# Second MLP product of an encoder block: half of the row-tile pairs by seven block products, two of the four weight sums formed by an accumulating load

## The chip, the cores and the metric

The kernel runs on one core of a Trainium2 chip. The metric is the device time of one execution in microseconds (us); smaller is better. The core has five engines that run beside each other, each with a queue of its own that it works through in order: PE (matrix products, accumulating in PSUM banks of 128x512 floats), DVE and ACT (elementwise work), POOL (GpSimd, elementwise work and issuing transfers) and SP (issues transfers). Transfers between HBM and the on-chip buffers run on 16 DMA engines.

## The reference

One post-norm encoder block on 256 tokens of width 2048, in float32:

```
mix = hybrid_mixer(x, ...)                                  # two kinds of attention
x = layer_norm(ALPHA * x + mix, ln1_g, ln1_b)
x = layer_norm(ALPHA * x + cross_attention(x, mem), ln2_g, ln2_b)
ff = square(relu(x @ w_mlp_in)) @ w_mlp_out                 # 2048 -> 8192 -> 2048
x = layer_norm(ALPHA * x + ff, ln3_g, ln3_b)
```

The change lies wholly in the MLP, and there in the product with `w_mlp_out`: a 256x8192 activation times an 8192x2048 matrix.

## The kernel before

**Precision.** Each product of two float32 matrices is made by three PE passes. Both operands are split into a high part (a copy in the type fp32r, made by ACT, L80) and a low part (the rest, source minus high part, made by DVE, L81); `mm3` (L146 to L148) adds high x high, high x low and low x high into one PSUM bank. So each 1024 columns of a weight cost one ACT and one DVE instruction before PE can use them. The split weights live in tiles `w_hi` and `w_lo` with four buffers each.

**The MLP.** The 8192 hidden columns are worked off in NCH = 4 chunks of CH = 16 column tiles of 128. Per chunk, four calls of `hidden_group` (L760) make the hidden activations `ht` (PE lines L195 and L200, then `hidden`, L730, squares and splits them). Then `pair_product(c, q)` (L804) multiplies the chunk's activations with the matching 2048 rows of `w_mlp_out`, for the left (q = 0) and the right (q = 1) half of the 2048 output columns. There are seven such calls: the last chunk's right half is made in another way (`proj_tokens`), so that the tail is short.

**Units.** A pair product runs over eight units p = 0 to 7. Unit p is a pair of row tiles (256 rows) by 1024 columns of the weight, laid out in HBM as one block of 128 partitions x 2048 floats, in the order B12, B11, B22, B21 of its four 128x512 blocks. The activation pair is a 2x2 block matrix A too (two token blocks by two row tiles). A plain unit makes all eight block products: 24 matmuls of 512 columns, into the banks x11, x12, x21, x22. It splits the weight in two parts of 1024 columns (`part`, L796). A unit for which `strassen(p)` holds (L745: p = 3 and p = 7) uses the Strassen-Winograd scheme: seven block products, 21 matmuls, of which four go to banks p1, p5, p6, p7 of their own. It needs four sums of activation blocks (s1 to s4 in `hidden`, L736 to L743: four DVE instructions on 128x128 and one split of 128x512 into `sums_h`) and four sums of weight blocks in a tile `s` of 2048 columns:

- columns 0 to 1023: B11 + B12 and B22 + B12, made by one DVE instruction over 1024 columns (L789),
- columns 1024 to 1535: (B11 + B12) + B22, one DVE instruction over 512 columns (L789),
- columns 1536 to 2047: that plus B21, one more over 512.

It splits four parts: `raw[512:1536]`, `raw[1536:2048]`, `s[0:1024]` and `s[1024:2048]`, that is 3584 columns in place of 2048. After the last unit, banks p1, p5, p6, p7 are copied out by ACT (L852) and added into the result rows `res` by DVE (L841, L844, L847).

**Loads.** `load_unit` (L775) takes the next unit: one transfer of 1 MB on SP's queue (L782). Units 0, 1, 4, 5 go to the two halves `raw2` of a fixed tile `wx`, the others to the three buffers of `raw`, which the first MLP product also uses. The two slots `sums_w` for `s` are the other half of `wx`. Two units are loaded ahead in program order.

**Order.** The tile framework plans the order of each engine's queue ahead of the run, from its own estimates of durations, within the dependencies; an instruction then waits at the head of its in-order queue until its inputs are there. Small DVE work that may wait is put in a list `side`: weight sums, the last additions into `res`, statistics. Each `part` takes one entry off it (`pump`), and a Strassen unit empties it first (L822).

Of the kernel before, what the change touches and what calls it, by code (L numbers as in the profile page):

```python
# [12 lines left out]
F32R = mybir.dt.float32r  # L13
BF16 = mybir.dt.bfloat16
AF = mybir.ActivationFunctionType
ALU = mybir.AluOpType
AX = mybir.AxisListType

P = 128
# [14 lines left out]
CH = 16  # L34
# [4 lines left out]
def encoder_kernel(ctx: ExitStack, tc: tile.TileContext, t, out):  # L39
    nc = tc.nc  # L40
# [19 lines left out]
    def f(ap):  # L60
        return ap.bitcast(F32)
# [7 lines left out]
    def tmp_tile():  # L69
        return tmp.tile([P, 512], F32, tag="tmp", name="tmp")  # L70
# [4 lines left out]
    def pin(ins, pinned):  # L75
        return tc.keep_in_program_order(ins) if pinned else ins

    def split(hi, lo, src, scale=None, pinned=False):
        if scale is None:
            pin(nc.scalar.activation(hi, src, AF.Copy), pinned)  # L80
            return pin(nc.vector.tensor_tensor(out=lo, in0=src, in1=f(hi), op=ALU.subtract), pinned)  # L81
        else:
            nc.scalar.activation(hi, src, AF.Copy, scale=scale)
            nc.vector.scalar_tensor_tensor(
                out=lo, in0=src, scalar=scale, in1=f(hi), op0=ALU.mult, op1=ALU.subtract)
# [9 lines left out]
    side = deque()  # L95

    def pump(n=1):

        for _ in range(n):
            if side:  # L100
                side.popleft()()
# [43 lines left out]
    def mm3(ps, ah, al, bh, bl, start, stop):  # L145
        nc.tensor.matmul(ps, ah, bh, start=start, stop=False)  # L146
        nc.tensor.matmul(ps, ah, bl, start=False, stop=False)  # L147
        nc.tensor.matmul(ps, al, bh, start=False, stop=stop)  # L148
# [289 lines left out]
    for b in range(NB):  # L438
# [3 lines left out]
        a, c, e = krn[:, 0:64], krn[:, 64:128], krn[:, 256:512]  # L442
        nc.vector.tensor_tensor(out=a, in0=v, in1=krt[:, 0, b, :], op=ALU.mult)
        for i in range(2):
            j = 1 - i
            nc.vector.tensor_tensor(out=c[:, i * 32:(i + 1) * 32], in0=v[:, j * 32:(j + 1) * 32],
                                    in1=krt[:, 1, b, i * 32:(i + 1) * 32], op=ALU.mult)
        nc.gpsimd.memset(e, 0.0)
        for par in range(2):
            dst = e[:, par * P:(par + 1) * P].rearrange("p (i g c) -> p i g c", g=2, c=32)  # L450
            nc.vector.tensor_tensor(
                out=dst[:, :, par, :], in0=a.rearrange("p (i c) -> p i c", c=32),
                in1=c.rearrange("p (i c) -> p i c", c=32), op=ALU.add)
# [41 lines left out]
    def stats_tile():  # L495
        return [small.tile([P, 5, 6], F32, tag="bn", name="bn"), 0]
# [81 lines left out]
    def big3(name):  # L578
        return big.tile([P, 8192], F32R, tag="big", name=name).rearrange("p (k c) -> p k c", c=512)
# [132 lines left out]

    early.close()
    late = ctx.enter_context(tc.tile_pool(name="late", bufs=1))
    s_in = Stream(t["w_mi"][4:])
    sts = [stats_tile() for _ in range(NB)]
    ht = big3("ht")
    sums_h = late.tile([P, 2048], F32R, name="sums_h").rearrange("p (u l c) -> p u l c", l=2, c=512)
    wx = big.tile([P, 8192], F32, tag="big", name="wx")
    raw2, sums_w = [[wx[:, o:o + 2048] for o in (i, i + 2048)] for i in (0, 4096)]  # L720

# [8 lines left out]
    def hidden(ps, j):  # L730

        r = []
        for i in range(2):
            r.append(square(ps[i]))
            split(ht[:, j + i, 0:S], ht[:, j + i, S:2 * S], r[i])
        if strassen(j // 2):  # L736
            (a11, a21), (a12, a22) = [(x[:, 0:P], x[:, P:S]) for x in r]
            s = tmp_tile()
            s1, s2, s3, s4 = [s[:, o:o + P] for o in range(0, 4 * P, P)]
            for o, a, b, op in ((s1, a21, a22, ALU.subtract), (s3, a11, a21, ALU.subtract),  # L740
                                (s2, s1, a11, ALU.subtract), (s4, a12, s2, ALU.add)):
                nc.vector.tensor_tensor(out=o, in0=a, in1=b, op=op)
            split(sums_h[:, j // 8, 0, :], sums_h[:, j // 8, 1, :], s)  # L743

    def strassen(p):  # L745
        return p % 4 == 3

    def last_weights(k):

# [10 lines left out]
    def hidden_group(nexts, tiles, j0):  # L760
# [7 lines left out]
        for i in range(0, G, 2):  # L768
# [1 line left out]

    units = [(c, q, p) for c in range(NCH) for q in range(2) for p in range(CH // 2)
             if not (c == NCH - 1 and q == 1)]
    loaded = deque()

    def load_unit(chunk):  # L775

        if not units or units[0][0] != chunk:
            return
        c, q, p = units.pop(0)
        seven = strassen(p)  # L780
        raw = raw2[p % 4] if p % 4 < 2 else raw_tile()
        nc.sync.dma_start(raw, t["w_mo"][(c * 2 + q) * (CH // 2) + p])  # L782
        s = None
        if seven:
            s = sums_w[p // 4 % 2]
            b12, b22, b21 = [raw[:, o:o + 512] for o in (0, 1024, 1536)]

            def add(out, a, b):
                side.append(lambda: nc.vector.tensor_tensor(out=out, in0=a, in1=b, op=ALU.add))  # L789
            add(s[:, 0:1024].rearrange("p (i c) -> p i c", i=2), raw[:, 512:1536].rearrange("p (i c) -> p i c", i=2),  # L790
                b12[:, None, :].broadcast_to([P, 2, 512]))
            add(s[:, 1024:1536], s[:, 0:512], b22)
            add(s[:, 1536:2048], s[:, 1024:1536], b21)
        loaded.append((raw, s))

    def part(src):  # L796
        w = src.shape[1]
        hi = wsp.tile([P, 1024], F32R, tag="w_hi", name="w_hi")
        lo = wsp.tile([P, 1024], F32R, tag="w_lo", name="w_lo")
        split(hi[:, :w], lo[:, :w], src)  # L800
        pump()
        return [(hi[:, o:o + 512], lo[:, o:o + 512]) for o in range(0, w, 512)]

    def pair_product(c, q):  # L804

        x11, x12, x21, x22 = [acc_tile() for _ in range(4)]
        p1, p5, p6, p7 = [att_tile() for _ in range(4)]
        n = CH // 2
        for p in range(n):
            load_unit(c)  # L810
            raw, s = loaded.popleft()
            k = 2 * p

            def a(k_, b):
                return ht[:, k_, b * P:(b + 1) * P], ht[:, k_, S + b * P:S + (b + 1) * P]

            def sm(i):
                return (sums_h[:, p // 4, 0, i * P:(i + 1) * P], sums_h[:, p // 4, 1, i * P:(i + 1) * P])

            if strassen(p):  # L820
                first, last = p == 3, p == n - 1
                pump(len(side))  # L822
                for src, todo in ((raw[:, 512:1536], ((p1, a(k, 0), first), (x12, sm(3), False))),
                                  (raw[:, 1536:2048], ((x11, a(k + 1, 0), False),)),
                                  (s[:, 0:1024], ((p5, sm(0), first), (p7, sm(2), first))),
                                  (s[:, 1024:2048], ((p6, sm(1), first), (x21, a(k + 1, 1), False)))):
                    for (hi, lo), (ps, (ah, al), start) in zip(part(src), todo):
                        mm3(ps, ah, al, hi, lo, start, last)
            else:
                for i in range(2):  # L830
                    w = part(raw[:, i * 1024:(i + 1) * 1024])
                    for (hi, lo), to in zip(w, ((x12, x22), (x11, x21))):
                        for b in range(2):
                            ah, al = a(k + i, b)
                            mm3(to[b], ah, al, hi, lo, p == 0 and i == 0, to[b] is x22 and p == n - 2 and i == 1)
        cols = [slice((2 * q + i) * 512, (2 * q + i + 1) * 512) for i in range(2)]
        r11, r12, r21, r22 = [res[b][:, cc] for b in range(NB) for cc in cols]

        def first_add(r, ps):
            if c == 0:  # L840
                nc.vector.scalar_tensor_tensor(out=r, in0=r, scalar=ALPHA, in1=ps,  # L841
                                               op0=ALU.mult, op1=ALU.add)
            else:
                nc.vector.tensor_tensor(out=r, in0=r, in1=ps, op=ALU.add)  # L844

        def add(o, x, y, op=ALU.add):
            side.append(lambda: nc.vector.tensor_tensor(out=o, in0=x, in1=y, op=op))  # L847

        first_add(r22, x22)
        m1, m5, m7, m6 = [tmp_tile() for _ in range(4)]  # L850
        for m, ps in ((m1, p1), (m5, p5), (m7, p7), (m6, p6)):
            nc.scalar.activation(m, ps, AF.Copy)  # L852
        first_add(r12, x12)
        first_add(r11, x11)
        first_add(r21, x21)
        add(r22, r22, m5)
        add(r12, r12, m5)
        add(m6, m1, m6)
        add(m7, m6, m7)
        add(r11, r11, m1)  # L860
        add(r12, r12, m6, ALU.subtract)
        add(r21, r21, m7)
        add(r22, r22, m7, ALU.subtract)
        if c == NCH - 1:
            for b, r in ((0, r11), (0, r12), (1, r21), (1, r22)):
                side.append(lambda b=b, r=r: stats(sts[b], r))

    for c in range(NCH):
        for g in range(CH // G):
            first = c == 0 and g == 0  # L870
# [27 lines left out]
    for b in range(NB):  # L898
# [10 lines left out]
        for i, c in enumerate(cols):  # L909
            if i + 1 < len(cols):  # L910
                shift(cols[i + 1])
            pin(nc.vector.scalar_tensor_tensor(
                out=res[b][:, c], in0=res[b][:, c], scalar=r, in1=b3[:, c],
# [119 lines left out]
```

## Time and profile before

| | |
|---|---|
| median of 3 runs | 1113.58 us (1113.04 to 1114.1) |
| the profiled execution | 1112.53 us |
| its span, first to last instruction | 1110.8 us |
| mean granted PE clock | 0.995 |
| matmuls | 5962 |
| MLP second product, seven pair products | about 42.2 us each |

The profile is one execution. "Busy" is the time in which an engine executes something; a matmul's own duration is longer than its distance to the next one, since matmuls are pipelined, so distances are read from start times. "SPq" is the queue of transfers that SP issues. "Granted clock" is the share of full PE speed that the throttle allowed.

### The profile page before, as it was taken

To read this page: it belongs to the slowest core of one execution; us is meant where nothing else is said; L and a number is where in the kernel's file an instruction comes from. 1 tells how busy PE (TensorE), PEld (TensorE's weight loads), DVE (VectorE), ACT (ScalarE), POOL (GpSimd) and SP (SyncE) were. 2 spreads that over 40 slices of the span, in tenths; PEclk is the share of its full clock that TensorE was granted. 3 is DMA by queue.
4 is the path that set the end of the run, shared out by engine and by line. 5 is a ranking of instruction groups with operands and counts; after the bars stand their busy time and mean duration, and the time that the engine had idled before them with its cause. 6 is when DMAs were issued, how large, how long until landed. Compare 5 with 4: busy or idle time off the path is not lost.

```text
span 1110.8 us, 15234 instructions
## 1 busy us (share of the span) xinstructions
PE 1095.6 (99%) x5962; PEld 946.3 (85%) x5962; DVE 828.1 (75%) x1202; ACT 574.1 (52%) x842; POOL 38.3 (3%) x45
## 2 busy tenths in 40 slices
PE   9999999999999989999999999999999999999996
PEld 6988899888998878888888888888888888888885
DVE  6878677687888777876976667868667777667695
ACT  6555565546576344544554445455445545554550
POOL 1402000000100000000000000000000000000000
PEclk9999999999999999999999999999999999999998
DMA  9654454466477427655456555555554565555372
GB/s 335 234 224 152 152 190 149 155 227 241 177 216 277 146 82 268 226 189 208 171 190 227 189 190 189 184 195 196 203 187 173 190 232 189 186 190 191 113 258 83
DMA packets 37944, 215.86 MB, mean 194 GB/s; under 512 B 4336, under 2 KB 5232, under 8 KB 14192
## 3 DMA queue, kind: packets, MB, share of 16 engines
q1 hardware_dynamic: 37872, 214.89, 54.5%
q8 instruction: 46, 0.75, 0.3%
q14 instruction: 26, 0.21, 0.1%
HBM read 212.78 MB, written 2.10 MB: 193 GB/s over the span
## 4 chain that ended last, share of the span: by engine, by line
PE 98%; DVE 1%; DMA 0%; issue 0%; ACT 0%; POOL 0%; DVEq 0%; SPq 0%
PE acc L147 16%; PE acc L146 16%; PE acc L148 16%; PE att L195 11%; PE acc L195 11%; PE att L200 5%; PE acc L200 5%; PE att L148 2%; PE att L147 2%; PE att L146 2%; PE acc L188 2%; PE acc L186 2%; PE acc L187 2%; PE att L535 1%; PE att L350 1%; PE att L362 0%
## 5 line engine op out<-in xcount | busy, mean ns | idle before, releaser
L81 DVE TENSOR_TENSOR w_lo<-raw,w_hi 128x1024 fp32r<-128x1024 f32 (+2 forms) x318 | 367.0, 1162 | 180.1 <-ACT w_hi L80 178.6
L80 ACT ACTIVATE w_hi<-raw 128x1024 fp32r<-128x1024 f32 (+2 forms) x318 | 320.0, 1013 | 333.6 <-PE acc L148 154.2
L147 PE MATMUL acc<-w_lo,ht 128*128 128x512 f32 x396 | 154.0, 389 | 0.0
L148 PE MATMUL acc<-w_hi,ht 128*128 128x512 f32 x396 | 154.0, 389 | 0.0
L195 PE MATMUL att<-x2t,w_hi 128*128 128x512 f32 x512 | 139.6, 394 | 0.0
L146 PE MATMUL acc<-w_hi,ht 128*128 128x512 f32 x396 | 136.0, 389 | 0.0
L195 PE MATMUL acc<-x2t,w_hi 128*128 128x512 f32 x480 | 132.3, 394 | 0.0
L80 ACT ACTIVATE w_hi<-wx 128x1024 fp32r<-128x1024 f32 x84 | 87.9, 1061 | 80.5 <-PE acc L148 59.7
L81 DVE TENSOR_TENSOR w_lo<-wx,w_hi 128x1024 fp32r<-128x1024 f32 x84 | 100.9, 1221 | 34.5 <-ACT w_hi L80 33.6
L195 PEld LDWEIGHTS att<-x2t,w_hi 128*128 128x128 f32 x512 | 88.1, 189 | 12.3
L195 PEld LDWEIGHTS acc<-x2t,w_hi 128*128 128x128 f32 x480 | 82.6, 189 | 11.5
L146 PEld LDWEIGHTS acc<-w_hi,ht 128*128 128x128 f32 x396 | 74.3, 188 | 15.5
L147 PEld LDWEIGHTS acc<-w_lo,ht 128*128 128x128 f32 x396 | 74.3, 188 | 15.4
L148 PEld LDWEIGHTS acc<-w_hi,ht 128*128 128x128 f32 x396 | 74.3, 188 | 15.4
L200 PEld LDWEIGHTS att<-x2t,w_lo 128*128 128x128 f32 x512 | 77.5, 189 | 10.2
L200 PEld LDWEIGHTS acc<-x2t,w_lo 128*128 128x128 f32 x480 | 73.3, 189 | 9.5
L200 PE MATMUL att<-x2t,w_lo 128*128 128x256 f32 x512 | 80.2, 281 | 0.0
L200 PE MATMUL acc<-x2t,w_lo 128*128 128x256 f32 x480 | 77.0, 281 | 0.0
L147 PE MATMUL acc<-w_lo,xt 128*128 128x512 f32 (+2 forms) x192 | 69.2, 362 | 0.0
L148 PE MATMUL acc<-w_hi,xt 128*128 128x512 f32 (+2 forms) x192 | 69.2, 361 | 0.0
L146 PE MATMUL acc<-w_hi,xt 128*128 128x512 f32 (+2 forms) x192 | 65.6, 361 | 0.5 <-ACT w_hi L80 0.5
L148 PE MATMUL acc<-w_hi,ot 128*128 128x512 f32 (+1 forms) x136 | 51.9, 382 | 0.0
(243 smaller groups left out, 1789.2 us busy)
## 6 DMA issues: line engine op xcount, KB each, us to landing
raw<-in_w_mi SPq DMA_DIRECT2D x64, 1024.0 KB, 4.8
wx<-in_w_mo SPq DMA_DIRECT2D x28, 1024.0 KB, 4.9
raw<-in_w_mo SPq DMA_DIRECT2D x28, 1024.0 KB, 4.8
raw<-in_w_out SPq DMA_DIRECT2D x16, 1024.0 KB, 4.9
raw<-in_w_ml SPq DMA_DIRECT2D x8, 1024.0 KB, 4.9
raw<-in_w_b SPq DMA_DIRECT2D x5, 1024.0 KB, 4.9
raw<-in_w_qa SPq DMA_DIRECT2D x16, 256.0 KB, 5.4
raw<-in_w_qa SPq DMA_DIRECT2D x4, 1024.0 KB, 4.9
```

Source lines behind the costliest of these rows:

```text
L80: pin(nc.scalar.activation(hi, src, AF.Copy), pinned)
L81: return pin(nc.vector.tensor_tensor(out=lo, in0=src, in1=f(hi), op=ALU.subtract), pinned)
L146: nc.tensor.matmul(ps, ah, bh, start=start, stop=False)
L147: nc.tensor.matmul(ps, ah, bl, start=False, stop=False)
L148: nc.tensor.matmul(ps, al, bh, start=False, stop=stop)
L186: nc.tensor.matmul(ps, hi, xt[:, k, 0:S], start=k == 0, stop=False)
L187: nc.tensor.matmul(ps, hi, xt[:, k, S:2 * S], start=False, stop=False)
L188: nc.tensor.matmul(ps, lo, xt[:, k, 0:S], start=False, stop=k == nk - 1)
L195: nc.tensor.matmul(ps, hi[:, i * P:(i + 1) * P], xt[:, k, :], start=k == 0, stop=k == nk - 1)
L200: nc.tensor.matmul(ps[:, 0:S], lo[:, i * P:(i + 1) * P], xt[:, k, 0:S], start=False, stop=False)
L350: nc.tensor.transpose(pp[:, st * S + b * P:st * S + b * P + P], ev[:, b, st * P:(st + 1) * P], ident)
L535: nc.tensor.transpose(ps[:, o:o + P], x(b, k // 4)[:, (k % 4 + j) * P:(k % 4 + j + 1) * P], ident)
```

## The change

Of the eight units of a pair product, p = 1, 3, 5 and 7 are now made by seven block products, in place of 3 and 7. `sums_h` grows from two to four sets of activation sums. Of the four weight sums, the first two are no longer made by DVE: B12 is loaded twice side by side into `s[0:1024]` by SP, and then a transfer issued by GpSimd adds B11 and B22 from HBM onto it. `raw` then holds only columns 512 to 2047 for such a unit. The other two sums remain DVE additions over 512 columns; they go to a list `sums` of their own, of which each `part` takes one entry ahead of `side`, and a seven-product unit empties that list but no longer `side`. Three units rather than two are loaded ahead in program order.

```diff
+    SEVEN = ((1, 3, 5, 7), (1, 3, 5, 7))
-    sums_h = late.tile([P, 2048], F32R, name="sums_h").rearrange("p (u l c) -> p u l c", l=2, c=512)
+    sums_h = late.tile([P, 4096], F32R, name="sums_h").rearrange("p (u l c) -> p u l c", l=2, c=512)
...
-        if strassen(j // 2):
+        if j // 2 in SEVEN[0]:
...
-            split(sums_h[:, j // 8, 0, :], sums_h[:, j // 8, 1, :], s)
-
-    def strassen(p):
-        return p % 4 == 3
+            u = SEVEN[0].index(j // 2)
+            split(sums_h[:, u, 0, :], sums_h[:, u, 1, :], s)
...
-    loaded = deque()
+    loaded, sums, slots = deque(), deque(), [0]
...
-        seven = strassen(p)
+        seven = p in SEVEN[q]
         raw = raw2[p % 4] if p % 4 < 2 else raw_tile()
-        nc.sync.dma_start(raw, t["w_mo"][(c * 2 + q) * (CH // 2) + p])
+        o = 512 if seven else 0
+        nc.sync.dma_start(raw[:, o:], t["w_mo"][(c * 2 + q) * (CH // 2) + p][:, o:])
         s = None
         if seven:
-            s = sums_w[p // 4 % 2]
-            b12, b22, b21 = [raw[:, o:o + 512] for o in (0, 1024, 1536)]
+            s = sums_w[slots[0] % 2]
+            slots[0] += 1
+            b22, b21 = raw[:, 1024:1536], raw[:, 1536:2048]
 
             def add(out, a, b):
-                side.append(lambda: nc.vector.tensor_tensor(out=out, in0=a, in1=b, op=ALU.add))
-            add(s[:, 0:1024].rearrange("p (i c) -> p i c", i=2), raw[:, 512:1536].rearrange("p (i c) -> p i c", i=2),
-                b12[:, None, :].broadcast_to([P, 2, 512]))
+                sums.append(lambda: nc.vector.tensor_tensor(out=out, in0=a, in1=b, op=ALU.add))
+            src = t["w_mo"][(c * 2 + q) * (CH // 2) + p]
+            nc.sync.dma_start(s[:, 0:1024].rearrange("p (i c) -> p i c", i=2),
+                              src[:, 0:512][:, None, :].broadcast_to([P, 2, 512]))
+            nc.gpsimd.dma_start(s[:, 0:1024], src[:, 512:1536], accum_op=ALU.add)
             add(s[:, 1024:1536], s[:, 0:512], b22)
             add(s[:, 1536:2048], s[:, 1024:1536], b21)
...
-        pump()
+        if sums:
+            sums.popleft()()
+        else:
+            pump()
...
-        n = CH // 2
-        for p in range(n):
-            load_unit(c)
+        plain = [p for p in range(CH // 2) if p not in SEVEN[q]]
+        for p in range(CH // 2):
+            for _ in range(2 if q == p == 0 else 1):
+                load_unit(c)
...
-            if strassen(p):
-                first, last = p == 3, p == n - 1
-                pump(len(side))
+            if p in SEVEN[q]:
+                first, last = p == SEVEN[q][0], p == SEVEN[q][-1]
+                while sums:
+                    sums.popleft()()
```

More of the change, by code (lines that the diff above doesn't have):

```diff
@@ L817, in sm @@
             def sm(i):
-                return (sums_h[:, p // 4, 0, i * P:(i + 1) * P], sums_h[:, p // 4, 1, i * P:(i + 1) * P])
-            if strassen(p):
-                first, last = p == 3, p == n - 1
-                pump(len(side))
+                u = SEVEN[0].index(p)
+                return sums_h[:, u, 0, i * P:(i + 1) * P], sums_h[:, u, 1, i * P:(i + 1) * P]
+            if p in SEVEN[q]:
+                first, last = p == SEVEN[q][0], p == SEVEN[q][-1]
+                while sums:
+                    sums.popleft()()
                 for src, todo in ((raw[:, 512:1536], ((p1, a(k, 0), first), (x12, sm(3), False))),
@@ L834, in pair_product @@
                             ah, al = a(k + i, b)
-                            mm3(to[b], ah, al, hi, lo, p == 0 and i == 0, to[b] is x22 and p == n - 2 and i == 1)
+                            mm3(to[b], ah, al, hi, lo, p == 0 and i == 0, to[b] is x22 and p == plain[-1] and i == 1)
         cols = [slice((2 * q + i) * 512, (2 * q + i + 1) * 512) for i in range(2)]
```

## The prediction, written before the run

> **What bounds the kernel now.** The page's busy times and the shares of the chain that ended last say which engine sets the end.
>
> ```profile
> PE 1095.6 (99%) x5962; PEld 946.3 (85%) x5962; DVE 828.1 (75%) x1202; ACT 574.1 (52%) x842; POOL 38.3 (3%) x45
> PE 98%; DVE 1%; DMA 0%; issue 0%; ACT 0%; POOL 0%; DVEq 0%; SPq 0%
> ```
>
> PE is busy for 99% of the span and makes 98% of the chain. But a share over the whole span says nothing of one stage, and "busy" can hide pauses. So the windows come next: the first two pair products, the four hidden groups between them and the next pair, and the last pair product.
>
> ```profile
> core 0: us, PE busy (x) PEld busy (x) DVE busy (x) ACT busy (x) POOL busy (x), PEclk, DMA share, GB/s
> 491.34:533.54 42.20, 42.20 (x188) 34.95 (x187) 32.84 (x45) 23.10 (x31) 0.00 (x0) 1.00 0.50 181
> 533.54:575.70 42.16, 42.16 (x188) 34.91 (x187) 31.92 (x37) 21.53 (x25) 0.00 (x0) 1.00 0.55 200
> 575.70:665.41 89.71, 89.71 (x514) 78.47 (x513) 62.10 (x89) 43.37 (x61) 0.00 (x0) 1.00 0.56 197
> ...
> 1013.50:1055.80 42.30, 42.30 (x188) 35.01 (x187) 30.42 (x42) 23.20 (x31) 0.00 (x0) 1.00 0.38 132
> ```
>
> A pair product takes 42.2 us, PE is busy for all of it at full clock, DVE for 32.84 (78%), ACT for 23.1, POOL for nothing, and the DMA engines are half used. Whether PE runs at its own pace is read from start times in PE's timeline: the first matmul of unit 0, the first of unit 3 (a seven-product unit), and one from behind it.
>
> ```profile
> 491.34 0.39 PE L146 MATMUL acc<-w_hi,ht 128*128 128x512 f32 x1
> ...
> 507.66 0.39 PE L146 MATMUL att<-w_hi,ht 128*128 128x512 f32 x1
> ...
> 512.65 0.84 PE L146 MATMUL acc<-w_hi,ht 128*128 128x512 f32 x3
> ```
>
> Units 0 to 2 are 3 x 24 = 72 matmuls: 16.32 us, 0.2267 us each. From 507.66 to 512.65 lie 22 (21 of unit 3 and one of unit 4 drawn ahead): 4.99 us, 0.2268 each. So the seven-product unit that exists already runs at the same pace without a pause, and the count closes the stage: 6 x 24 + 2 x 21 = 186 matmuls x 0.2267 = 42.17 us. A plain unit is 5.44 us, a seven-product unit 4.76.
>
> That the splits keep up, the waits within the two pair products show.
>
> ```profile
> ACT w_hi L80 <- PE acc L148: 39.6, 27, 3.4
> DVE w_lo L81 <- ACT w_hi L80: 18.4, 15, 2.5
> ...
> DVE wx L789 <- DMA raw<-in_w_mo: 0.7, 2, 0.4
> ```
>
> ACT waits 39.6 us for PE to give back one of the four `w_hi` buffers, DVE waits for ACT, nobody but one weight sum waits for a transfer. The splits run as far ahead as the buffers allow. **PE's count of matmuls is the bound**, in this stage as elsewhere.
>
> **The change, part by part.**
>
> *Matmuls.* Each pair product turns two plain units into seven-product ones: 2 x 3 matmuls fewer. With seven pair products, 42 x 0.2267 = **9.52 us** go from PE, as long as PE stays the bound. A pair product becomes 42.20 - 1.36 = 40.84 us.
>
> *DVE and ACT.* Two DVE instructions in a row are closer than their durations, so I take distances between starts, with the durations of the rarer ones as an upper bound.
>
> ```profile
> 532.37 2.36 DVE L81 TENSOR_TENSOR w_lo<-wx,w_hi 128x1024 fp32r<-128x1024 f32 x2
> 534.64 1.89 DVE L847 TENSOR_TENSOR res<-res,tmp 128x512 f32<-128x512 f32 x3
> 536.45 0.68 DVE L841 SCALAR_TENSOR_TENSOR res<-res,acc 128x512 f32<-128x512 f32 x1
> ```
> ```profile
> L80 ACT ACTIVATE w_hi<-raw 128x1024 fp32r<-128x1024 f32 x280 | 295.4, 1061 | 302.9 <-PE acc L148 126.5 <-PE acc L195 77.7 <-PE att L195 55.5
> ...
> L80 ACT ACTIVATE w_hi<-raw 128x512 fp32r<-128x512 f32 x30 | 18.8, 633 | 24.2 <-PE acc L148 21.2 <-DMA raw<-in_w_qa 2.4
> ...
> L742 DVE TENSOR_TENSOR tmp<-tmp 128x128 f32<-128x128 f32 x32 | 9.2, 286 | 0.3
> ...
> L81 DVE TENSOR_TENSOR sums_h<-tmp,sums_h 128x512 fp32r<-128x512 f32 x8 | 5.5, 686 | 0.0
> ```
>
> 1024 columns cost DVE (534.64 - 532.37)/2 = 1.135 us, 512 columns (536.45 - 534.64)/3 = 0.60. Per pair product: the two sums over 1024 columns go (-2.27); two units split 3584 columns in four parts for 2048 in two, so one split of 1024 and one of 512 more each (+2 x 1.735 = 3.47); and they need two sums over 512 each (+2.40). Net +3.6: DVE 32.84 to 36.4 us of 40.84, 89%. ACT gets 2 x (1.061 + 0.633) = 3.4 more: 26.5 of 40.84. Both stay below PE, which hides them; if DVE were the bound, the stage would have to hold 4.4 us more DVE work than this. In the hidden groups, two more sets of activation sums per chunk cost DVE 2 x (4 x 0.286 + 0.686) = 3.7 us and ACT 1.3, beside 62.10 busy of 89.71: no time.
>
> *Transfers.* These rows price them.
>
> ```profile
> q1 hardware_dynamic: 37872, 214.89, 54.5%
> ...
> wx<-in_w_mo SPq DMA_DIRECT2D x28, 1024.0 KB, 4.9
> raw<-in_w_mo SPq DMA_DIRECT2D x28, 1024.0 KB, 4.8
> ```
> ```profile
> L782 SPq DMA_DIRECT2D wx<-in_w_mo x28: 327/328/414, 422.9 to 1017.0; - x28
> L782 SPq DMA_DIRECT2D raw<-in_w_mo x28: 327/328/328, 472.4 to 1021.6; - x28
> ...
> DMA to landing us min/median/max: 4.6/4.8/12.2
> ```
>
> 214.89 MB took 54.5% of 1110.8 us: 2.82 us per MB, 2.95 for a 1 MB block (1.049 million bytes). A seven-product unit now moves 3/4 block into `raw` (2.2), half a block as the doubled B12 (1.5) and half a block that is added (1.5 if it costs what a copy does). A pair product: 4 x 2.95 + 4 x 5.2 = 32.5 us of 40.84, 80%. The trace shows no accumulating transfer. It reads HBM and its own target, so twice its bytes is the other bound: 2.95, then 38.4 us, 94%. Even that is no limit for the stage, since the trace shows some units loaded before it starts (the first issues to `wx` at 422.9 and to `raw` at 472.4, against 491.34).
>
> The Trainium skill has a rule here ("Collectives: The Full Stack", Part 3, the bandwidth ceiling): an add within a transfer costs two source reads on one ring and so runs at half the rate of a copy. No run here shows it yet; by it, the 94% would hold rather than the 80%, and the sum would stay.
>
> *Latency.* The new chain is: slot of `s` free, SP's load of B12, its landing, GpSimd's transfer, its landing, two DVE sums, split. A slot comes back every second seven-product unit, 2 x (5.44 + 4.76) = 20.4 us. It is free when the last part of its unit is split, one ACT (1.06) and one DVE instruction (1.14) behind the start of that unit, when the buffer comes free. The third part of its next unit is wanted by PE 9 matmuls (2.04) behind that unit's start, and its split takes 2.2. So the chain has 20.4 - 2.2 - 0.2 = 18.0 us. I take 4.9 us for each landing, the row of 1 MB: the accumulating one reads 0.5 + 0.5 MB. That makes 9.8, **8 us to spare**. Bounds for the accumulating transfer: at least a quick landing, 4.6; at most the longest of this tensor, 12.2, with which the chain still fits by 0.9. By the Trainium skill ("DMA: Bandwidth & Descriptors", anatomy of the GpSimd path), such a transfer is estimated at 2.0 us plus bytes over 436 GB/s, 3.2 us for this one; no run shows it, and the sum doesn't use it.
>
> *Issues and queues.* SP issues one more transfer per seven-product unit (28 x 0.33 us) in a queue that mostly waits for buffers; the load of B12 waits there for its slot, with later units' loads behind it, each wanted over 10 us later. GpSimd, idle in the stage, issues 28 and waits for each B12; nothing else stands in its queue. The new waits on DVE are the delicate ones: a sum over 512 columns stands in the in-order queue with the next units' splits behind it, and PE waits for those.
>
> *The sum.* 1112.53 - 9.52 = 1103.0 for the profiled execution (1.73 outside its span, unchanged). It lies 1.05 under the median, so against 1113.58: **1104.1 us**.
>
> **The rivals.**
>
> *A, a part is lost at the start of the stage* (0.12). Unit 1 is now a seven-product unit while DVE still has the last hidden activations to work off, and it has 1.7 + 1.2 us more to do there. If PE waits 1 to 2 us in each of four chunks: 1108 to 1112. For it: the first pair product has DVE at 32.84, the fuller one. Against it: PE has no pause there now, and the buffers give two parts ahead.
>
> *B, slower: the accumulating load lands later than the planned order assumes* (0.28). Then a sum blocks DVE's queue. Behind it waits the split of the next plain unit's first half: its buffer comes free 6 matmuls (1.36) into the seven-product unit, it is ready 2.2 later, and PE wants it at 4.76, so 1.2 us of slack; a part further on has 4.6. With 2 us as the slack, each seven-product unit loses (delay - 2.0). The first two of each chunk load early, leaving 28 - 8 = 20. Time = 1104.1 + 20 x (delay - 2.0); it decides from a delay of 2.5 us, where the loss eats the 9.5. If the plan assumes 4.9, that is a landing of 7.4; at 8.6 the time is 1138, at 9.8 (two reads one after the other) 1162. For it: no such transfer has been seen, and the DMA share rises to 80 to 94%. Against it: today's sums wait for their load 0.4 us at most in these two stages.
>
> *C, no gain* (0.08): four parts through four buffers take as long as a plain unit, 5.44 us; then 14 x 0.68 is lost and the time is 1113.6. The pace of 0.2268 in unit 3 speaks against it, though three plain units stand before that one, and only one would now.
>
> **How the numbers follow.** The forecast gets 0.52. A measurement of this kernel tells about 0.2% (2.2 us) from no change. Faster: the forecast and most of A, 0.62. Within 0.2%: C and the end of A, 0.10. Slower: B, 0.28. The range starts a little under the forecast, 1102.5 (the pace of PE bounds it), takes in A and C, and reaches into B to 1130, where a little over half of B (0.15) and 0.03 below are left out. The forecast's own range is 1103 to 1107.
>
> **What would show it.** Right: 42 matmuls fewer, pair products of 40.9 us with PE busy throughout, a pace of 0.227 in units 1 and 5, DVE near 36 us per stage, DMA share 0.8 to 0.95, and `wx` sums that wait for a transfer under 2 us. Wrong: PE pauses in seven-product units, with DVE idle before a sum on 512 columns released by a transfer (B), pauses only around the first unit 1 of each chunk (A), or a pitch above 0.227 with ACT and DVE waiting for each other (C).

## The result and the profile after

| | median us | runs | span of the profiled execution |
|---|---|---|---|
| before, same chip | 1113.84 | 1113.04 to 1114.27 | 1110.8 |
| changed | 1211.22 | 1208.41 to 1213.59 | 1206.4 |

The ratio is 1.0874, interval 1.0857 to 1.0891: 97 us slower, where 9.5 us faster was forecast and the range ended at 1130. The side was that of rival B; the size was not.

First the page of the changed kernel: busy times, PE and its granted clock by slices, the transfer queues, the chain that ended last, and the landing of GpSimd's transfers.

```profile
PE 1121.5 (93%) x5920; PEld 954.5 (79%) x5920; DVE 861.7 (71%) x1284; ACT 599.9 (50%) x878; POOL 62.8 (5%) x73
...
PE   9999999999999999977899987799998779999896
...
PEclk9999999999999999988899988899999889999998
...
q1 hardware_dynamic: 45488, 222.23, 53.1%
q0 software_dynamic: 4032, 14.68, 6.9%
...
PE 67%; DMA 20%; DVE 9%; issue 2%; ACT 1%; SPq 0%; POOL 0%; POOLq 0%; DVEq 0%; ACTq 0%
...
wx<-in_w_mo SPq DMA_DIRECT2D x28, 512.0 KB, 4.5
wx<-in_w_mo POOLq DMA_DIRECT2D x28, 512.0 KB, 8.7
```

The matmuls are 42 fewer, as forecast (5962 to 5920), yet the chain has 20% of DMA and 9% of DVE in it. PE has holes in three places and a shorter one at the end: the three chunks with two pair products and the last with one. No engine is full: DVE fell from 75% to 71%, the 16 engines are busy for 60%. So this is latency, not rate. The windows of a pair of products, of the hidden groups behind it, and of the last product:

```profile
core 0: us, PE busy (x) PEld busy (x) DVE busy (x) ACT busy (x) POOL busy (x), PEclk, DMA share, GB/s
493.00:606.10 113.10, 91.85 (x362) 72.20 (x361) 71.13 (x92) 51.22 (x63) 6.06 (x7) 0.91 0.65 191
606.10:696.40 90.30, 89.88 (x513) 78.27 (x513) 64.89 (x98) 44.26 (x63) 0.87 (x1) 1.00 0.60 204
...
1106.50:1152.00 45.50, 41.76 (x183) 33.80 (x181) 33.22 (x47) 26.17 (x35) 1.74 (x2) 1.00 0.51 155
```

A pair of products takes 113.1 us; 362 matmuls at 0.2267 would be 82.1. Of the 31 us between, 21.25 is idle PE, and 9.8 is PE busy at a lower clock (0.91).

Where PE waits, DVE's timeline shows. Its rows from the first left half to the right one:

```profile
511.38 6.36 DVE L81 TENSOR_TENSOR w_lo<-wx,w_hi 128x1024 fp32r<-128x1024 f32 x6
527.35 1.42 DVE L790 TENSOR_TENSOR wx<-wx,raw 128x512 f32<-128x512 f32 x2 [9.61 <-DMA wx<-in_w_mo]
528.69 2.35 DVE L81 TENSOR_TENSOR w_lo<-wx,w_hi 128x1024 fp32r<-128x1024 f32 x2
530.96 3.49 DVE L81 TENSOR_TENSOR w_lo<-raw,w_hi 128x1024 fp32r<-128x1024 f32 x3
535.02 0.69 DVE L81 TENSOR_TENSOR w_lo<-raw,w_hi 128x512 fp32r<-128x512 f32 x1 [0.57 <-ACT w_hi L80]
543.72 1.42 DVE L790 TENSOR_TENSOR wx<-wx 128x512 f32<-128x512 f32 x2 [8.01 <-DMA wx<-in_w_mo]
545.06 1.22 DVE L81 TENSOR_TENSOR w_lo<-wx,w_hi 128x1024 fp32r<-128x1024 f32 x1
```

At 527.35 stand the two sums of unit 7. DVE waited 9.61 us for their accumulating load. The next two splits are the third and fourth part of **unit 5**, which PE wants first: the sums of the unit after next stand ahead of them in the queue. SP's and GpSimd's issues close the circle (start, duration, idle before and what ended it):

```profile
512.63 0.38 SPq L792 DMA_DIRECT2D wx<-in_w_mo  x1
...
529.93 0.38 SPq L792 DMA_DIRECT2D wx<-in_w_mo  x1
...
546.30 0.38 SPq L792 DMA_DIRECT2D wx<-in_w_mo  x1
```
```profile
517.62 0.86 POOL L794 DMA_DIRECT2D wx<-in_w_mo  x1 [13.46 <-DVE w_lo L81]
534.70 0.86 POOL L794 DMA_DIRECT2D wx<-in_w_mo  x1 [16.22 <-DVE w_lo L81]
551.09 0.86 POOL L794 DMA_DIRECT2D wx<-in_w_mo  x1 [15.52 <-DMA wx<-in_w_mo]
567.52 0.87 POOL L794 DMA_DIRECT2D wx<-in_w_mo  x1 [15.57 <-DMA wx<-in_w_mo]
```

The third split of unit 5 (528.69, 1.14 us) frees a slot of `s` at 529.83; SP loads B12 into it at 529.93; GpSimd issues at 534.70 (4.8 us later); the sums that wait for it start at 543.72 (9.0 later) and take 1.34; behind them comes the third split of the next seven-product unit, 1.14; it frees the other slot, and SP issues at 546.30. That is 16.4 us a turn, and GpSimd's starts are 16.4 us apart from 534.70 to 583.91. Two slots were meant to be two chains side by side. The place of the sums in DVE's queue ties them into one chain, and each seven-product unit with its plain one takes a turn of 16.4 us in place of 10.2.

### The profile page after: what moved, and what is told of

It reads as the page before. It is cut to its first block, busy times and chain, and to the rows that moved or that the text cites. A ratio compares the mean times of both kernels' runs of the same rounds, so it can differ in the third digit from the quotient of the medians.

```text
span 1206.4 us, 15438 instructions
## 1 busy us (share of the span) xinstructions
PE 1121.5 (93%) x5920; PEld 954.5 (79%) x5920; DVE 861.7 (71%) x1284; ACT 599.9 (50%) x878; POOL 62.8 (5%) x73
## 3 DMA queue, kind: packets, MB, share of 16 engines
q1 hardware_dynamic: 45488, 222.23, 53.1%
q0 software_dynamic: 4032, 14.68, 6.9%
## 4 chain that ended last, share of the span: by engine, by line
PE 67%; DMA 20%; DVE 9%; issue 2%; ACT 1%; SPq 0%; POOL 0%; POOLq 0%; DVEq 0%; ACTq 0%
DMA wx<-in_w_mo 19%; PE acc L195 10%; PE att L195 10%; PE acc L147 8%; PE acc L148 8%; PE acc L146 8%; DVE w_lo L81 6%; PE acc L200 5%; PE att L200 5%; PE acc L188 2%; PE acc L186 2%; PE acc L187 2%; PE att L147 2%; PE att L148 2%; DVE wx L790 2%
## 5 line engine op out<-in xcount | busy, mean ns | idle before, releaser
L80 ACT ACTIVATE w_hi<-wx 128x1024 fp32r<-128x1024 f32 x112 | 111.3, 1005 | 161.1 <-PE acc L148 101.9
L81 DVE TENSOR_TENSOR w_lo<-wx,w_hi 128x1024 fp32r<-128x1024 f32 x112 | 126.3, 1154 | 26.6 <-ACT w_hi L80 26.3
L147 PE MATMUL acc<-w_lo,ht 128*128 128x512 f32 x312 | 125.4, 402 | 0.2
L148 PE MATMUL acc<-w_hi,ht 128*128 128x512 f32 x312 | 124.5, 399 | 0.0
L147 PE MATMUL att<-w_lo,sums_h 128*128 128x512 f32 x84 | 42.2, 503 | 67.9 <-DVE w_lo L81 67.9
L146 PE MATMUL acc<-w_hi,ht 128*128 128x512 f32 x312 | 104.3, 412 | 0.3
L200 PEld LDWEIGHTS att<-x2t,w_lo 128*128 128x128 f32 x512 | 77.5, 189 | 10.2
L147 PEld LDWEIGHTS att<-w_lo,sums_h 128*128 128x128 f32 x84 | 19.1, 228 | 81.5 <-DVE w_lo L81 78.0
L146 PEld LDWEIGHTS acc<-w_hi,ht 128*128 128x128 f32 x312 | 63.3, 204 | 15.8 <-ACT w_hi L80 1.6
L147 PEld LDWEIGHTS acc<-w_lo,ht 128*128 128x128 f32 x312 | 60.8, 195 | 15.0 <-DVE w_lo L81 1.7
L790 DVE TENSOR_TENSOR wx<-wx 128x512 f32<-128x512 f32 x28 | 19.3, 690 | 73.0 <-DMA wx<-in_w_mo 72.8
L148 PEld LDWEIGHTS acc<-w_hi,ht 128*128 128x128 f32 x312 | 60.8, 195 | 13.2
```

What stands on the lines that cost most here:

```text
L200: nc.tensor.matmul(ps[:, 0:S], lo[:, i * P:(i + 1) * P], xt[:, k, 0:S], start=False, stop=False)
L790: sums.append(lambda: nc.vector.tensor_tensor(out=out, in0=a, in1=b, op=ALU.add))
```

## The experiments

The theory from the trace is this **closed loop**. Its rivals: the accumulating load or the DMA engines are too slow whatever the order (**transfer rate**), and four seven-product units are too much for DVE (**DVE work**).

**1. The order alone.** The two sums go behind the second split of their own unit; the plan may not move them ahead of it (an ordering edge without a wait). Loads and work are unchanged.

```diff
-        if sums:
-            sums.popleft()()
-        else:
-            pump()
+        pump()
...
+                    if i == 2:          # the third part of a seven-product unit comes next
+                        for _ in range(2):
+                            sums.popleft()()
```

> The changed kernel with one difference: the two DVE sums of a seven-product unit stand in DVE's queue behind the second split of that same unit, no longer ahead of the splits of the unit two before it. Same matmuls, same transfers. Theory 'closed loop' (a sum that stands early in DVE's queue blocks the third split of the unit before, that split frees the slot of s for the next accumulating load, so each seven-product unit takes the whole chain of 16.4 us, not 10.2): the loop is open, the chain of about 15 us fits the 18 us between two uses of a slot, 1104 to 1108 us. Rival 'transfer rate' (the accumulating load at 8.7 us, or the DMA engines, set the pace whatever the order): 1180 or more. Rival 'DVE work' (four seven-product units are more than DVE can do in 40.8 us): 1130 or more.

Measured: 1112.62 us, ratio to before 0.9987 (0.9977 to 0.9996). 98.6 us (1211.22 - 1112.62) go with the order of 56 DVE instructions (a few entries of `side` move with them). The accumulating load still lands in 8.2 us and SP's load of B12 in 8.0, later than the 4.5 of the changed kernel, with the DMA engines busier (84%, against 65%):

```profile
493.54:578.00 84.46, 82.53 (x362) 67.37 (x361) 73.57 (x94) 50.22 (x63) 6.07 (x7) 1.00 0.84 251
```

So the closed loop stands and the two rivals fall as causes of the slowdown. But 1104 to 1108 was missed: 84.46 us for a pair of products is no less than before, with 360 matmuls in place of 372. 360 x 0.2267 would be 81.6, so some 2.8 us are missing, in each of three chunks: PE is idle for 1.9 of them and slow around that. A second cause was left, and experiments 5 to 12 look for it.

**2. All sums on DVE**, one whole load per unit, no GpSimd. The sums stand as early in DVE's queue as in the changed kernel.

```diff
-            nc.sync.dma_start(s[:, 0:1024]..., src[:, 0:512][:, None, :].broadcast_to([P, 2, 512]))
-            nc.gpsimd.dma_start(s[:, 0:1024], src[:, 512:1536], accum_op=ALU.add)
+            add(s[:, 0:1024]..., raw[:, 512:1536]..., b12[:, None, :].broadcast_to([P, 2, 512]))
```

> The changed kernel with four seven-product units per pair product, but all weight sums on DVE as in the kernel before and one whole 1 MB load per unit; no accumulating load. DVE work per pair product: 32.84 + 3.47 + 2 x (1.135 + 1.2) = 41.0 us against 40.84 us of PE. Theory 'closed loop': the chain of two transfers is gone, so 1104 to 1114, DVE full. Rival 'transfer rate': the same. Rival 'DVE work': 1130 or more.

Measured: 1114.53 us, ratio 0.9999 (0.9989 to 1.0008), half a microsecond above the forecast's upper end. Without an accumulating load the early place in the queue makes nothing 97 us slower. But DVE is at 79.27 of 84.40 us, and nothing is gained.

**3. Two seven-product units, sums by loads.** Only `SEVEN = ((3, 7), (3, 7))` differs from the changed kernel.

> The changed kernel with only units 3 and 7 by seven products, as in the kernel before, but with their sums by the accumulating load. Work on PE as before. Theory 'closed loop': one seven-product unit in 21.1 us, longer than the 16.4 us of the loop, so 1112 to 1118. Rival 'transfer rate' taken as a price per accumulating load (97 + 9.5 us over 28 loads = 3.8 us each): 14 of them, about 1167.

Measured: 1113.4 us, ratio 0.9994 (0.9984 to 1.0003). Fourteen accumulating loads cost nothing where a turn has 21 us, though their sums stand early here too. A price per load would have given 1167.

**4. Copy instead of add** in the changed kernel (`accum_op` left out; the sums lack B12).

> The changed kernel with the GpSimd-issued load copying instead of adding, so the weight sums lack B12. Everything else as in the changed kernel, the double load of B12 included. It measures what the adding costs. Theory 'closed loop': the period falls by as much as the landing does; if the copy lands in 4.5 us (the 512 KB load of SP) instead of 8.7, the period is 12.2 us, 2 us over the 10.2 of PE, and the time 1104 + 17 x 2 = about 1138. If GpSimd's issue rather than the adding is slow, the landing stays near 8.7 and the time near 1211. Rival 'transfer rate' with the adding as its price: 1104 to 1115.

Measured: 1162.91 us in one run. GpSimd's copy and its queue:

```profile
q0 software_dynamic: 4032, 14.68, 4.1%
...
wx<-in_w_mo POOLq DMA_DIRECT2D x28, 512.0 KB, 5.8
```

```profile
531.95 0.54 POOL L794 DMA_DIRECT2D wx<-in_w_mo  x1 [15.62 <-DVE w_lo L81]
544.88 0.54 POOL L794 DMA_DIRECT2D wx<-in_w_mo  x1 [12.40 <-DMA wx<-in_w_mo]
558.89 0.54 POOL L794 DMA_DIRECT2D wx<-in_w_mo  x1 [13.46 <-DVE w_lo L81]
572.05 0.54 POOL L794 DMA_DIRECT2D wx<-in_w_mo  x1 [12.62 <-DVE w_lo L81]
```

The copy lands in 5.8 us, so adding costs 2.9. GpSimd's starts are 12.9, 14.0 and 13.2 us apart, 13.4 in the mean and 3 less than with adding: the turn follows the landing, as a closed loop must. I had expected the landing of SP's 512 KB load, 4.5, and so 1138. The changed kernel lost (1211 - 1104) us at 6.2 a turn (16.4 - 10.2), as many as 17 turns; 17 turns at 3.2 (13.4 - 10.2) make 54 us, so 1158. That sum was made after the run.

**5. The late additions held back.** In the first experiment PE pauses in unit 1 of the right half. DVE's queue there, then PE's:

```profile
538.16 1.22 DVE L81 TENSOR_TENSOR w_lo<-wx,w_hi 128x1024 fp32r<-128x1024 f32 x1
539.29 0.69 DVE L858 TENSOR_TENSOR tmp<-tmp 128x512 f32<-128x512 f32 x1
539.90 0.68 DVE L81 TENSOR_TENSOR w_lo<-wx,w_hi 128x512 fp32r<-128x512 f32 x1
540.50 0.69 DVE L791 TENSOR_TENSOR wx<-wx 128x512 f32<-128x512 f32 x1
541.10 0.68 DVE L858 TENSOR_TENSOR tmp<-tmp 128x512 f32<-128x512 f32 x1
541.71 0.68 DVE L858 TENSOR_TENSOR res<-res,tmp 128x512 f32<-128x512 f32 x1
542.31 1.22 DVE L81 TENSOR_TENSOR w_lo<-wx,w_hi 128x1024 fp32r<-128x1024 f32 x1
```
```profile
541.82 0.61 PE L146 MATMUL att<-w_hi,sums_h 128*128 128x512 f32 x2
543.58 0.50 PE L147 MATMUL att<-w_lo,sums_h 128*128 128x512 f32 x1 [1.14 <-DVE w_lo L81]
```

DVE doesn't stop once; three of the late additions (L858) stand between the splits, and PE gets its low part at 543.5 instead of 542.3. This is the **seam** between the two halves: four first additions, eight late ones, and the splits of units 7, 0 and 1 in a row. The edit holds the eight behind the splits of unit 2 and later.

```diff
+            hold[0] = q == 1 and p < 2      # and in part(): pump() only if not hold[0]
...
-            side.append(lambda: nc.vector.tensor_tensor(out=o, in0=x, in1=y, op=op))
+            def go():                       # ordered behind the split made last, for the left half
+                ins = nc.vector.tensor_tensor(out=o, in0=x, in1=y, op=op)
```

> As the kernel with the sums behind their own split (1112.62 us), and the eight late additions into the result rows (the entries of the list side after the left half's pair product) don't run before unit 2 of the right half's pair product, held there in DVE's queue. Same matmuls, transfers and DVE work. In that kernel PE pauses for 2.8 us near unit 1 of the right half, in each of three chunks, 8.4 us, which is nearly all that is missing to 1104. Theory 'seam' (at the change from left to right half, DVE has four first additions, eight late additions and the splits of three seven-product units within four; the late ones stand ahead of a split that PE waits for): 1104 to 1106. Rival 'first additions or transfers' (the four first additions that free PSUM, or the accumulating load of unit 1, make the pause): 1110 to 1113. Rival 'pace' (PE does not go faster with fewer matmuls, the stage stays at 84.5 us): 1112 to 1114.

Measured: 1110.04 us, ratio 0.9961 (0.9949 to 0.9974). The pause in unit 1 is gone, though the edit moves neither the first additions nor the accumulating load of unit 1; one of about 1.4 us has come up in unit 3, where four additions now stand. So the late additions made that pause. But 1104 to 1106 is missed again, and the time is one that the rival "first additions or transfers" (1110 to 1113) forecast: the place of the pauses speaks against that rival, the time does not.

**6. The same with all sums on DVE** (experiment 2 with the additions held back).

> As the kernel with all weight sums on DVE (1114.53 us), with the late additions held back to unit 2 of the right half. DVE was busy for 79.3 us of a pair of products there, and PE needs 81.6. Theory 'seam': most of the pause goes though DVE is nearly full, 1105 to 1110. Rival 'DVE work' (at 79.3 of 81.6 us DVE cannot follow, so the sums must leave it): 1111 to 1115, and then the accumulating loads are worth what lies between this run and the one with loads.

Measured: 1110.98 us, ratio 0.9971 (0.9962 to 0.998), against 0.9999 without the hold. Between the two theories' numbers, but the hold gains 3.5 us here as well, with no accumulating load in the kernel. So the pause at the seam does not need the loads. And after both repairs, the loads are worth 0.9 us, no more than the runs spread.

**7. Additions in plain units only.**

> As the kernel with the additions held back to unit 2, and they are taken in splits of plain units alone (2, 4, 6 of the right half, two entries each, the rest in the next hidden group). Theory 'seam': no more to gain than by holding them back to unit 2, within 1.5 us of it, 1104 to 1106; if DVE is short near units 3 and 5 too, this one is faster by 1 to 3 us. Rivals 'first additions or transfers' and 'pace': 1110 to 1114.

Measured: 1112.97 us, ratio 0.999 (0.9981 to 0.9999). A miss, inside the rivals' 1110 to 1114: two of the eight are left over, and PE's pauses appear at the start of the next hidden groups, about 2.2 us per chunk.

**8. Additions spread**: two in each of units 2, 4, 6, one at the end of units 3 and 5.

> As the kernel with the additions held back to unit 2 of the right half (1110.04 us), but not one behind every split from there: two in plain units 2, 4 and 6, one at the end of units 3 and 5, so that the eight are done by unit 6. Holding them back moved PE's pause from unit 1 to unit 3, where four of them came within one seven-product unit: DVE then has 7.5 + 6 x 0.6 = 11.1 us of work in a pair of units that PE does in 10.2. With three per pair of units it is 9.3. Theory 'seam' (DVE is short for a while wherever the additions crowd, not over the whole): no pauses over 0.3 us in units 1 and 3, 1104 to 1107. Rival 'loads' (what is left of the pauses is the accumulating load landing late): 1109 to 1111, with the pauses where they are.

Measured: 1109.64 us, ratio 0.9956 (0.9943 to 0.9968), the fastest here of the kernels with whole sums, 4.5 us under the kernel before it on the same chip. The time misses the theory's 1104 to 1107 and lies in the rival's 1109 to 1111; the pauses in units 1 and 3, which the rival expected to stay, are gone in the first two chunks, and one of 0.7 us is left in unit 3 of the third. The window of its first pair of products (364 matmuls, against 362 in experiment 1's) has PE idle for 0.3 us in place of 1.9.

```profile
492.87:576.60 83.73, 83.42 (x364) 67.62 (x362) 73.98 (x95) 50.21 (x63) 6.07 (x7) 1.00 0.84 250
```

**9. One addition per unit**, from unit 0.

> As the kernel with the additions spread, but one at the end of each of the eight units from unit 0, the thinnest spread: 7.5 + 1.2 = 8.7 us of DVE work per pair of units, but two of them within the first two units, where the four first additions are (2.5 us). Theory 'seam': within 2 us of the other spread, 1104 to 1108, any pause being in units 0 and 1. Rival 'loads': 1109 to 1111.

Measured: 1111.24 us, ratio 0.9976 (0.9967 to 0.9985). A little outside both forecasts. In the first pair of products PE starts late at 564, in the middle of the right half, where it waits for one of ACT's splits, and at 578, where the hidden groups start, for one of DVE's; units 0 and 1, where two of the additions now stand, show no pause. So thinner is not better. Ahead of the pause at 564, DVE's first sum waited 1.35 us for its accumulating load (at 560.04), and ACT then waited for the second sum before it could split the fourth part.

**10. The end of a product behind its last split**, and **11. also the right half's additions held behind single splits of the hidden groups**, the one on top of experiment 8, the other on top of both. In experiment 8, ACT waits at the head of its queue for bank p1 and makes the wanted split afterwards:

```profile
571.89 0.60 ACT L873 ACTIVATE tmp<-att 128x512 f32<-128x512 f32 x1 [3.02 <-PE att L148]
572.63 1.06 ACT L80 ACTIVATE w_hi<-wx 128x1024 fp32r<-128x1024 f32 x1
```

```diff
-            nc.scalar.activation(m, ps, AF.Copy)
+            behind(nc.scalar.activation(m, ps, AF.Copy), last_hi[0])
...
+            if ps is not x22:
+                behind(ins, last_lo[0])
```

> As the kernel with the additions spread (1109.64 us), and at the end of each pair product the copies of banks p1, p5, p6, p7 (ACT) and three of the four first additions (DVE) stand behind the last split of unit 7. In that kernel PE pauses for about 1.2 us at the end of each right half: ACT waits 3.0 us at the head of its queue for bank p1 and only then makes the split that PE needs next, and DVE has two first additions ahead of that split. Theory 'seam': that pause goes in up to three chunks, 1105.5 to 1108. Rival: the copies now free the banks late, and PE waits for a bank at the start of the next product: 1109 to 1112.

> As the kernel with the end of the product behind the last split, and the late additions of the right half are held behind one split of the next hidden group each. Theory 'seam': DVE has one addition per 2.8 us of PE there and PE's waits at the start of the hidden groups go (0.3 to 0.5 us per chunk): equal to that kernel or up to 1.5 us faster. Rival 'loads': no change within 0.5 us.

Measured: 1110.66 us (0.9978, 0.9969 to 0.9986) and 1111.82 us (0.998, 0.9971 to 0.9989). Neither is faster than experiment 8. The first lies in its rival's range (1109 to 1112), but the waits of PE that the profile names there are for splits, not for a bank. By PE's start times the pauses at the end of the right half are 1.7 to 1.8 us per chunk, longer than the 1.2 of experiment 8, so the copies of the banks are not what these 1.2 us hang on.

The queues show what the wanted split waits for. It is the split of unit 7's fourth part, which needs the second weight sum. DVE's rows of experiment 8, then ACT's of experiment 10:

```profile
569.51 0.69 DVE L792 TENSOR_TENSOR wx<-wx,raw 128x512 f32<-128x512 f32 x1
570.12 1.22 DVE L81 TENSOR_TENSOR w_lo<-wx,w_hi 128x1024 fp32r<-128x1024 f32 x1
571.25 0.68 DVE L857 SCALAR_TENSOR_TENSOR res<-res,acc 128x512 f32<-128x512 f32 x1
571.85 0.68 DVE L792 TENSOR_TENSOR wx<-wx,raw 128x512 f32<-128x512 f32 x1
```
```profile
574.95 1.06 ACT L82 ACTIVATE w_hi<-wx 128x1024 fp32r<-128x1024 f32 x1 [3.80 <-DVE wx L794]
```

The second sum stands behind the third part's split and a first addition, and ends at 572.53, just ahead of ACT's split at 572.63: whatever the order of the bank copies, that split could start no earlier. In the first pair of products of experiments 10 and 11, where the copies stand behind the split, ACT waits 3.8 us ahead of it, until that sum is there. At the end of the left half in experiment 8's first pair the two sums stand side by side (from 527.55), and PE has no pause there. No run moves the second sum alone, so this cause is read from the traces and not tested.

**12. Experiment 8 with a copy instead of an add** (the sums lack B12).

> As the kernel with the additions spread (1109.64 us), with GpSimd's load copying instead of adding, so the weight sums lack B12. It shows what the adding still costs once the loop is open. Theory 'closed loop' (the landing only counts where something is queued behind it): within 1.5 us of 1109.6. Rival 'loads' (the rest of the missing gain is the landing of the accumulating load): 1104 to 1107.

Measured: 1107.89 us, ratio 0.995 (0.9935 to 0.9965), 1.75 us under experiment 8, between the two forecasts. The sums' waits for a transfer, in experiment 8 and then here:

```profile
L792 DVE TENSOR_TENSOR wx<-wx,raw 128x512 f32<-128x512 f32 x28 | 19.2, 686 | 2.9 <-DMA wx<-in_w_mo 2.8
L792 DVE TENSOR_TENSOR wx<-wx 128x512 f32<-128x512 f32 x28 | 19.2, 686 | 0.8 <-DMA wx<-in_w_mo 0.4
```
```profile
L792 DVE TENSOR_TENSOR wx<-wx 128x512 f32<-128x512 f32 x28 | 19.2, 684 | 0.2
L792 DVE TENSOR_TENSOR wx<-wx,raw 128x512 f32<-128x512 f32 x28 | 19.1, 683 | 0.1
```

In experiment 8 the sums waited 3.7 us in all, here 0.3. With the loop open, an add that lands 2.2 us later (7.9 against 5.7) is worth 1.75 us in all; in the closed loop 2.9 us of landing were worth 48 (1211 to 1163). In PE's start times of this run, 1.1 us per chunk are still missing, all at the end of the right half, in three chunks. 1107.9 - 3.3 = 1104.6: close to the forecast's sum. So the place of the last missing 3.3 us is known; their cause, the late second sum, is only read from the queues.

## Why the prediction was wrong, by its own steps

**Matmuls: right.** 42 fewer, and the pace of 0.2267 holds; the last product, which has no seam behind it, needs 180 matmuls in place of 186: from its first start on these take 40.81 us in experiment 1 and 42.17 before, 1.36 us less, as forecast.

**Latency: the size was off, and the step was built wrongly.** The accumulating landing measured 8.7 us, not the 4.9 taken from the row of 1 MB; the chain from slot to sum is 14 us, not 9.8. That alone did no harm: it fits the 18.0 us worked out between two uses of a slot. In experiment 1 the two landings make even 16.2 us (8.0 and 8.2), and the 56 sums wait 3.5 us in all. The 3.2 us that the prediction cites for such a transfer, without using them, were not met by any run here: even the plain copy took 5.7. **The step that failed** is that those 18.0 us assumed two slots that run side by side. I listed the new sums as "the delicate ones" in DVE's queue, and yet counted the slot's return by PE's units, not by the instruction that returns it, which stands in that same queue. (It is the third part's split, not the last one's as I had counted: SP issues at 529.93, 0.1 us behind its end.)

**Rival B named the place and priced it as an open loop.** "Delay minus 2.0 us of slack" per unit makes a late landing cost its lateness. The chain is closed over the two slots, so a unit costs the whole turn, 16.4 us against 10.2. It also took the next plain unit's split for the blocked one; it was the third split of the unit before, the one that frees the slot. At a landing of 7.4 its price only eats the gain; at the 8.7 measured it gives 1140, where 1211 was measured. Nor did it count PE's clock: 9.8 of the 31 us lost in the first pair of products.

**DVE work: right on the mean, wrong for the place.** 36.4 us per product was forecast, 73.57 / 2 = 36.8 measured in experiment 1. But "89%, hidden" is a mean over 40 us. At the seam DVE has no idle time from 531.2 to 551.2 in experiment 1's timeline, 20 us in a row, and that kernel kept only 1.5 of the 9.5 us (1114.08, the kernel before on the same chip, less 1112.62). Rival A saw a crowd, and put it at the start of the left half; it was between the halves.

**Transfers: right.** A share of 80 to 94% was forecast and 84% measured, and it bounds nothing. The rule of the Trainium skill that was weighed ("Collectives: The Full Stack", Part 3, the bandwidth ceiling: an add within a transfer reads twice and runs at half rate, told there of the adds in a ReduceScatter) agrees with the queue rows: 14.68 MB took 6.9% of 1206.4 us in the changed kernel, 5.7 us per MB, against 2.9 for SP's queue (222.23 MB in 53.1%). GpSimd's plain copy took 4.1% of 1160.9 us, 3.2 per MB.

**Rival C** (a slow pace of the seven-product unit) is out: in experiment 12 the first pair of products runs from 492.11 to 572.15, where its last pauses begin, without a pause: 80.04 us, which is 353 matmuls at 0.2267, seven whole seven-product units and most of the eighth among them.

## What to carry to other kernels

When an instruction that waits for a transfer enters an in-order queue, look for the instruction behind it that frees the buffer of the next such transfer: if it stands behind it in the same queue, the buffers don't overlap, and as soon as the chain (here 16.4 us) is longer than the work of a turn (10.2), the price is the whole chain per turn, not the lateness. Where a turn had 21 us, the same order cost nothing. Put such an instruction just ahead of its first user rather than as early as the plan allows; here that was worth 98.6 us. And a free share of 11% over a stage did not hide what met at one point of it: read the longest stretch without idle time, not the mean.

## What the runs showed of the hardware

**A long pause costs PE twice.** Behind the 7.4 us between these starts, PE goes on at 0.43 us per matmul, half its pace; the windows below give its granted clock behind the pause and a little later.

```profile
522.55 0.61 PE L146 MATMUL att<-w_hi,sums_h 128*128 128x512 f32 x2
529.96 0.80 PE L147 MATMUL att<-w_lo,sums_h 128*128 128x512 f32 x1 [6.79 <-DVE w_lo L81]
530.56 0.63 PE L148 MATMUL att<-w_hi,sums_h 128*128 128x512 f32 x1
530.98 0.63 PE L147 MATMUL att<-w_lo,sums_h 128*128 128x512 f32 x1
```
```profile
529.90:533.20 3.30, 3.24 (x8) 2.56 (x9) 3.30 (x4) 1.06 (x1) 0.00 (x0) 0.50 0.49 128
533.40:537.00 3.60, 3.60 (x17) 2.93 (x17) 1.74 (x2) 0.77 (x2) 0.86 (x1) 1.00 0.68 238
```

The Trainium skill ("TensorE: Matmul & The Clock Gate", Part 1) has the PE clock at half after an idle window of about 3.4 us and back after as much work; the clock of 0.50 for some 3.3 us here agrees. The short pauses, 1.9 us of idle time in experiment 1's window and 0.3 in experiment 8's, left it at 1.00 (the rows above). A pause under 3.4 us did it here too: in the changed kernel PE was idle for 2.77 us up to 562.71 and for 0.52 up to 564.45, and its clock was 0.55 from 564.4 to 567.8.

**An accumulating load of 512 KB issued by GpSimd** occupied GpSimd for 0.87 us and landed in 7.9 to 9.5 us; the same as a copy, 0.55 and 5.7 to 5.8.
